# The hand-over into and out of the attention of a hybrid attention and RG-LRU block: other order of the first loads, other slots, earlier loads for the next stage

## The chip, the core and the metric

The kernel runs on one core of a Trainium2 chip. The metric is the device time of one launch in microseconds (us). The engines are TensorE (PE, matmuls; its weight loads are listed as PEld), VectorE (DVE), ScalarE (ACT), GpSimd (POOL) and SyncE (SP, which here only issues DMAs). Each engine works through its own instructions in the order in which the program writes them; engines wait for each other by semaphores. The tile framework is used with a manual schedule: the order on each engine is the order of the calls in the code.

## The reference

One decoder block over 2048 positions of width 1024:

```python
proj = x @ w_in + b_in            # q, k, v of 24 heads (3 groups of 8), g_attn, u_lru, g_lru, two merge gates
q, k = rope(q), rope(k)
for g, (window, dilation) in enumerate(((128, 1), (512, 4), (2048, 16))):
    # query t sees keys t - j*dilation, j = 0..128: blocks of 128 queries against [previous, own] block of keys
    o_g, lse_g = dilated_band_attention(q[:, :, g], k[:, :, g], v[:, :, g], window, dilation)
attn = sum(softmax(lse over g) * o_g) * silu(g_attn)
y_a  = attn @ w_attn_proj                                  # 512 -> 1024
h    = rg_lru(causal_depthwise_conv(u_lru), ...)           # scan over positions
y_b  = (h * silu(g_lru)) @ w_lru_proj                      # 1024 -> 1024
merged = sigmoid(gA) * y_a + sigmoid(gB) * y_b
out  = layer_norm(ALPHA * x + merged @ w_out + b_out)
```

## The kernel before

All products are float32 in accuracy: an operand is split into a high part in the format that PE multiplies in one pass (fp32r) and a low part, the rest, and a product is three matmuls (high x high, high x low, low x high). A split is one ACT activation (the high part) and one subtraction on DVE or POOL (the low part).

Four stages follow each other, with PE the busiest engine in each.

**Projection** (to 1463 us). Writes q (already split: `qh`, `ql`), k, v, the gates and h = the LRU's output times its gate to scratch tensors in device memory. In its last pieces of work (the counter j of the last sequence step) the dictionary `begin` (L882) issues the attention's first loads on SP.

**Attention** (1463 to 1768 us). There are 12 units u = 0..11; a unit is a group g = (0, 2, 1)[u % 3] with two of its heads (a pair hp = u // 3), over 16 blocks of 128 queries. The main loop (L1071) takes a pair of blocks each round, its index j being 8 a unit. A round writes, in this order: the tasks that have come due (`run(late)`), the score products of this pair (`scores`, PE, L953), `weigh` of its first block (DVE adds the mask and takes the row's minimum, L966; ACT takes the exp, L968), the PE transposes of the p of the round two before (`turn_p`, L982) and their copies out of PSUM (`copy_p`, ACT L995, every third time also ACT, else DVE L997, for the second half), `weigh` of the second block, and the products with V of the round three before (`values`, L1013). A finished group of four blocks goes to `o_scr` by a POOL DMA. The counter `now["n"]` rises by one with each block, so by two a round; `later(lag, fn)` puts fn on a list that `run(late)` calls when lag blocks have gone by.

A unit needs three things: q (`A`, 2 MB in four transfers, `q_parts` L811), raw k (`C`, 1 MB in two transfers, `k_parts` L780), split into `B` and the rest in place (`k_split`, two pieces of a POOL cast L799 and a POOL subtraction L800; for unit 0 on ACT and DVE), and V (four transfers, `v_parts`; one V tile holds two head pairs of a group).

**yb** (1768 to 1970 us). 32 jobs n = 8c + f, `yb_job` L1214: chunk c of 512 positions, f a block of 128 output columns, 8 x 3 matmuls each (L1223 to L1225). Its weights W_f1 are loaded and split by `prep_wl(f)`, two splits of 128 x 512 a tile (L1043), its h by `load_h(c, k)`, one split each (L1040 and, for c = 0, the rest on POOL). `prep_wl(0)`, `prep_wl(1)` and `load_h(0, 0..7)` are called in unit 11 of the attention, the others in this stage, `prep_wl(f)` for f = 2..7 at job f - 2. Beside it run the 16 `combine` calls, that normalise and add the three groups' o (DVE L1150, POOL L1152 to L1154), transpose them on PE (L1159) and gate them. In the last jobs the next stage's operands are prepared: `prep_wa`, `prep_wo` and `load_at`.

**ya and output** (1970 to 2228 us). `ya_job` (L1298 to L1300), the merge, `out_job` with W_out, and the layer norm.

The large tiles live in slots of fixed size, X0 to X5 for the whole program, Y0 to Y3 for the attention, Z0 to Z3 after it. A tile that takes a slot waits, at its first write, for the last reader of the tile that had it before. The tenants named in this text:

- `QSLOT` (X3, X1, Y0) and `KSLOT` (X4, Y3) for A and B; `VSLOT` (L760) for V; raw k (`KR`, L777) in X2 and X5 by turns, two units to a tile.
- `prep_wl` (L1048): W_f1 tiles f = 0, 1 in X2, then 2, 3 in X0, 4, 5 in X1, 6, 7 in X5.
- `prep_wo` (L1183): W_out tiles in Z2 (k = 0, 1), X0 (2, 3), X1 (4, 5), X5 (6, 7). Job 28 is the first to call it for k = 2.

Raw loads pass through `rc` tiles (L1035), 4 buffers in the attention.

```python
    def prep_wo(k, j):
        if k % 2 == 0 and j == 0:
            WO["t"] = big(("Z2", "X0", "X1", "X5")[k // 2], [P, 2, 2, D], F32R, f"wo{k}")
```

Of the kernel before, what the change touches and what calls it, by code (L numbers as in the profile page):

```python
# [8 lines left out]
F32 = mybir.dt.float32  # L9
F32R = mybir.dt.float32r  # L10
# [5 lines left out]
P = 128  # L16
S = 2048
# [14 lines left out]
def hybrid_block_kernel(ctx: ExitStack, tc: tile.TileContext, a: dict, out: bass.AP):  # L32
# [73 lines left out]
    def later(lag, fn):  # L106
        late.append((now["n"] + lag, fn))
# [649 lines left out]
    at(base[len(seq)] + 12, lambda: load_cs(1))  # L757

    QSLOT, KSLOT = ("X3", "X1", "Y0"), ("X4", "Y3")
    VSLOT = {(0, 0): "X0", (2, 0): "Y1", (1, 0): "Y2", (0, 1): "X0", (2, 1): "Y1", (1, 1): "Y2"}  # L760
    KR = {}

    units = {}
# [5 lines left out]
    def k_parts(u):  # L769

        g, hp = unit(u)
        src = qk_scr["k", 4 * g + hp].rearrange("(d h) s -> h d s", h=2)

        def part(h, hs):
            def fn():
                if h == 0 and u % 2 == 0:
                    KR["t"] = big(("X2", "X5")[u // 2 % 2], [P, 2, S], F32R, f"C{u}")  # L777
                if h == 0:
                    units[u] = [None, None, KR["t"][:, u % 2]]
                sp.dma_start(flat(units[u][2][hs]), src[h])  # L780
            return fn

        return [part(0, lo_), part(1, up_)]
# [95 lines left out]
            at(max(t, 0), fn)  # L879

    firstv = v_parts(0, 0)
    begin = {0: k_parts(0), 1: q_parts(0), 2: k_parts(1), 4: firstv[:1], 5: firstv[1:]}  # L882
    low = NS
    where = [(s, j) for s in range(NQ) for j in range(ticks[s])]
    for T, (s, j) in enumerate(where):
# [147 lines left out]
    cur = {"rc": at_p}  # L1033

    def rc(name):  # L1035
        return cur["rc"].tile([P, CH], F32, tag="rc", name=name, bufs=(4 if cur["rc"] is at_p else 6))

    def split(h, l, r, scale=None, eng=dve):
        if scale is None:
# [3 lines left out]
            act.activation(h, r, AF.Copy, scale=scale)  # L1043
            dve.scalar_tensor_tensor(out=l, in0=r, scalar=scale, in1=flat(h), op0=ALU.mult, op1=ALU.subtract)

    def prep_wl(f):
        if f % 2 == 0:
            WL["t"] = big(("X2", "X0", "X1", "X5")[f // 2], [P, 2, 2, 8, P], F32R, f"wl{f}")  # L1048
        t = WL[f] = WL["t"][:, f % 2]
        for j in range(2):  # L1050
            ks = slice(4 * j, 4 * j + 4)
            r = rc(f"wlr{f}{j}").rearrange("p (k f) -> p k f", f=P)
            sp.dma_start(r, a["w_f1"][f, :, 4 + 4 * j:8 + 4 * j, :])
            later(1, lambda r=r, ks=ks: split(t[:, 0, ks], t[:, 1, ks], r, 0.5))

    def load_h(c, k):
        if k % 4 == 0:
            HH["t"] = big((("X3", "X4"), ("Z0", "Z1"))[c % 2][k // 4], [P, 4, 2, CH], F32R, f"h{c}{k}")
        t = HH[c, k] = HH["t"][:, k % 4]
        r = rc(f"hr{c}{k}")  # L1060
        sp.dma_start(r, hb_scr[k * P:(k + 1) * P, c * CH:(c + 1) * CH])
        eng = pool if c == 0 else dve
        later(1 if c else 2, lambda: split(t[:, 0], t[:, 1], r, eng=eng))

    NB = 12 * 16
    for fn in q_parts(1) + v_parts(2, 0) + k_parts(2):
        fn()
# [3 lines left out]
    for j in range(NJ + 3):  # L1071
        u, n0 = divmod(2 * j, 16)
        run(late)
        if j < NJ:
            scores(j)
            weigh(2 * j)
        if 2 <= j < NJ + 2:
            turn_p(j - 2)
            copy_p(j - 2, 0)
            copy_p(j - 2, 1)  # L1080
        if j < NJ:
            weigh(2 * j + 1)
        if j >= 3:
            values(j - 3)
        for n in (n0, n0 + 1):
            if 1 <= n <= 2 and u <= 10:
                k_split(u + 1, n - 1)
            if n == 0 and 1 <= u <= 9:
                loads += k_parts(u + 2)
            if n == 0 and u <= 9:  # L1090
                loads += q_parts(u + 2)
            if n == 7 and u in VORD:
                loads += v_parts(*VORD[u])
            if loads:
                loads.pop(0)()
            if u == 11 and n in (1, 2):
                prep_wl(n - 1)
            if u == 11 and 3 <= n < 11:
                load_h(0, n - 3)
            now["n"] += 1  # L1100
            if n == n0:
                run(late)
# [357 lines left out]
```

## Time and profile before

| | |
|---|---|
| runs before | 2216.63, 2217.81, 2247.49 us (median 2217.81) |
| profiled execution | 2229.57 us; span of the profile 2227.8 us |
| mean granted TensorE clock over the span | 0.986 of full speed |

| stage | us | PE busy us | granted clock | DMA share |
|---|---|---|---|---|
| projection | 0 to 1463 | 1452.18 | 1.00 | 0.75 |
| attention | 1463 to 1768 | 297.54 | 0.91 | 0.77 |
| yb | 1768 to 1970 | 199.99 | 0.99 | 0.80 |
| ya and output | 1970 to 2228 | 246.48 | 0.99 | 0.40 |

The granted clock is the rate that the chip's throttle allows TensorE, as a share of full speed. The DMA share is the mean busy share of the core's 16 DMA engines. In the rows below, a line of the timeline reads: start in us, length in us, engine, source line, operation, written tile <- read tiles, shapes, count, and in brackets the idle time just before with what ended it. A row of the windows view reads: stretch, its length, then busy time and count of PE, PEld, DVE, ACT and POOL, then the granted clock, the DMA share and the GB/s moved.

### The profile page before, as it was taken

What the parts mean: (1) busy time and instruction counts of PE and PEld (TensorE: products, weight loads), DVE (VectorE), ACT (ScalarE), POOL (GpSimd) and SP (SyncE); (2) the same over time, 40 slices, a digit from 0 to 9 for tenths busy, and PEclk for the clock granted to TensorE, in tenths of its full rate; (3) what the DMA queues carried; (4) which work ended last, traced back from release to release, by engine and by line L of the source; (5) the groups of instructions that cost most, each with busy time, mean ns of one, the idle gap of its engine ahead of it and who ended that gap; (6) DMA issues with size and microseconds to landing.
All of it is one profiled execution on the core that took longest, in us unless ns stands there. A gap on an engine that the chain in (4) does not pass through costs nothing. (4 is left out here: it accounts for less than half of the span.)

```text
span 2227.8 us, 35342 instructions
## 1 busy us (share of the span) xinstructions
PE 2196.2 (99%) x12016; PEld 1848.7 (83%) x12016; DVE 1742.7 (78%) x3242; ACT 1198.4 (54%) x2171; POOL 715.4 (32%) x559
## 2 busy tenths in 40 slices
PE   8999999999999999999999999999999999999998
PEld 6888888888887888888888888889999878888786
DVE  7888898899998777787788878747776377877677
ACT  5456466656566566667677776647776411121100
POOL 1555455455554011111111111114433246621220
PEclk9999999999999999999999999989999699999999
DMA  6977977977977766586576776699984389864431
GB/s 211 261 233 213 273 229 222 273 216 247 278 235 224 254 193 200 187 231 191 185 216 195 229 204 209 209 260 280 263 240 121 124 293 291 254 215 146 156 123 66
DMA packets 295524, 481.75 MB, mean 216 GB/s; under 512 B 90176, under 2 KB 122976, under 8 KB 290736
## 3 DMA queue, kind: packets, MB, share of 16 engines
q1 hardware_dynamic: 275888, 437.61, 63.4%
q0 software_dynamic: 14128, 32.19, 7.0%
q10 hardware_dynamic: 5328, 9.70, 1.2%
q8 instruction: 95, 1.56, 0.3%
q14 instruction: 85, 0.70, 0.1%
HBM read 303.17 MB, written 176.23 MB: 215 GB/s over the span
## 5 line engine op out<-in xcount | busy, mean ns | idle before, releaser
L614 PE MATMUL q<-xT,hS 128*128 128x512 f32 x1632 | 503.9, 390 | 1.3 <-DVE y L230 1.3
L614 PE MATMUL q<-xB,hA 128*128 128x512 f32 x1344 | 417.3, 392 | 9.1 <-ACT xB L218 8.5
L614 PE MATMUL q<-xT,l 128*128 128x512 f32 x1088 | 423.6, 389 | 0.0
L614 PE MATMUL q<-xB,l 128*128 128x512 f32 x944 | 368.4, 390 | 0.0
L614 PEld LDWEIGHTS q<-xT,hS 128*128 128x128 f32 x1632 | 305.4, 188 | 64.5 <-issue 1.7
L614 PEld LDWEIGHTS q<-xB,hA 128*128 128x128 f32 x1344 | 252.3, 189 | 62.3 <-ACT xB L218 8.5
L614 PEld LDWEIGHTS q<-xT,l 128*128 128x128 f32 x1088 | 204.2, 188 | 42.7
L614 PEld LDWEIGHTS q<-xB,l 128*128 128x128 f32 x944 | 177.7, 188 | 37.4
L968 ACT ACTIVATE p<-p,osb 128x256 f32<-128x256 f32 (+1 forms) x384 | 154.9, 453 | 87.3 <-DVE osb L966 86.7
L230 POOL TENSOR_TENSOR sw<-sw,sin 128x512 f32<-128x512 f32 x96 | 153.7, 1623 | 122.6 <-ACT sw L318 99.7
L230 POOL TENSOR_TENSOR y<-y,h 128x512 f32<-128x512 f32 x28 | 40.2, 1437 | 412.8 <-DVE h L517 336.8
L1013 PE MATMUL o<-V,ptb 128*128 128x65 f32 x1200 | 169.7, 297 | 2.5 <-DMA V<-v_scr 2.5
L614 PE MATMUL q<-xB,hS 128*128 128x512 f32 x544 | 168.6, 391 | 0.3 <-DVE v L230 0.3
L614 PE MATMUL q<-xT,hA 128*128 128x512 f32 x544 | 168.1, 390 | 0.1
L1013 PEld LDWEIGHTS o<-V,ptb 128*128 128x128 f32 x1200 | 156.2, 208 | 9.4 <-DMA V<-v_scr 2.6
L966 DVE CUSTOM_DVE_ANT_0 p<-s,mask 128x256 f32<-128x256 f32 (+1 forms) x384 | 121.7, 362 | 46.7 <-PE s L953 46.5
L274 ACT ACTIVATE hA<-wA 128x512 fp32r<-128x512 f32 x220 | 138.7, 635 | 21.2 <-PE g L483 6.6
L274 ACT ACTIVATE hS<-S 128x512 fp32r<-128x512 f32 x170 | 108.5, 638 | 61.9 <-DVE S L230 55.0
L230 POOL TENSOR_TENSOR l<-wA,hA 128x512 fp32r<-128x512 f32 x68 | 107.9, 1587 | 81.5 <-ACT hA L274 58.6
L614 PEld LDWEIGHTS q<-xT,hA 128*128 128x128 f32 x544 | 101.7, 188 | 21.4 <-issue 0.5
L614 PEld LDWEIGHTS q<-xB,hS 128*128 128x128 f32 x544 | 101.3, 188 | 21.3 <-issue 0.7
L230 DVE TENSOR_TENSOR y<-y,cos 128x512 f32<-128x512 f32 x96 | 106.6, 1117 | 0.0
(197 smaller groups left out, 4651.9 us busy)
## 6 DMA issues: line engine op xcount, KB each, us to landing
wA<-in_w_in_dram SPq DMA_DIRECT2D x219, 256.0 KB, 4.6
wl_scr<-l SPq DMA_DIRECT2D x102, 512.0 KB, 4.9
l<-wl_scr SPq DMA_DIRECT2D x102, 512.0 KB, 4.0
wS<-in_w_in_dram SPq DMA_DIRECT2D x102, 256.0 KB, 4.1
wS<-in_w_in_dram POOLq DMA_DIRECT2D x68, 256.0 KB, 7.2
mg_scr<-y SPq DMA_DIRECT2D x59, 256.0 KB, 4.9
o_scr<-osb POOLq DMA_DIRECT2D x48, 264.0 KB, 8.0
oc<-o_scr SPq DMA_DIRECT2D x48, 264.0 KB, 4.9
```

What stands on the lines that cost most here:

```text
L230: eng.tensor_tensor(out=out, in0=in0, in1=in1, op=op)
L274: act.activation(heads(h), heads(r, False), AF.Copy)
L614: pe.matmul(bank, w[:, ks], x[:, kk, xx], start=(first and i == 0), stop=(last and i == 11))
L966: dve.tensor_tensor_reduce(out=p[:, h, lo:256], in0=bank[h][:, m % 2, lo:256], in1=mask[:, lo:256], scale=1.0, scalar=3e38, op0=ALU.add, o ...
L968: act.activation(p[:, h, lo:256], p[:, h, lo:256], AF.Exp, scale=-1.0, bias=mm)
L1013: pe.matmul(o[:, b, h * 65:h * 65 + 65], ptb[:, b, 2 * h + x, :], V[:, kb, vo + h * 65:vo + h * 65 + 65], start=(x == lo // P), stop=(x == 1))
```

## The change

It has four parts.

1. The first loads. `begin` issues V for unit 0 ahead of unit 1's raw k. So that V need not wait for a slot that is still in use, V of group 0 moves from X0 to X5, and the raw k tiles that used X5 move to X0.
2. The copies of p. In rounds j = 2, 3, 4 of the attention, `weigh` of the pair's first block comes behind `turn_p` and `copy_p`, not ahead of them.
3. The next stage's first operands. `prep_wl` can do one half of a tile (`js`); the halves of W_f1 tile 0 are called in unit 10, as are the first four `load_h`; the other four `load_h` and tile 1 are called in unit 11. Each call stands in a round of its own, and its split follows six blocks (three rounds) behind the load, where it was one or two blocks. `rc` has 5 buffers in place of 4 in the attention.
4. W_f1's tiles exchange slots: f = 2, 3 in X5, f = 6, 7 in X0. `prep_wo`'s table is as before.

```diff
-    VSLOT = {(0, 0): "X0", (2, 0): "Y1", (1, 0): "Y2", (0, 1): "X0", (2, 1): "Y1", (1, 1): "Y2"}
+    VSLOT = {(0, 0): "X5", (2, 0): "Y1", (1, 0): "Y2", (0, 1): "X5", (2, 1): "Y1", (1, 1): "Y2"}
...
-                    KR["t"] = big(("X2", "X5")[u // 2 % 2], [P, 2, S], F32R, f"C{u}")
+                    KR["t"] = big(("X2", "X0")[u // 2 % 2], [P, 2, S], F32R, f"C{u}")
...
-    begin = {0: k_parts(0), 1: q_parts(0), 2: k_parts(1), 4: firstv[:1], 5: firstv[1:]}
+    begin = {0: k_parts(0), 1: q_parts(0), 3: firstv[:2], 4: firstv[2:], 5: k_parts(1)}
...
-        return cur["rc"].tile([P, CH], F32, tag="rc", name=name, bufs=(4 if cur["rc"] is at_p else 6))
+        return cur["rc"].tile([P, CH], F32, tag="rc", name=name, bufs=(5 if cur["rc"] is at_p else 6))
...
-    def prep_wl(f):
-        if f % 2 == 0:
-            WL["t"] = big(("X2", "X0", "X1", "X5")[f // 2], [P, 2, 2, 8, P], F32R, f"wl{f}")
-        t = WL[f] = WL["t"][:, f % 2]
-        for j in range(2):
+    def prep_wl(f, js=(0, 1)):
+        if js != 1:
+            if f % 2 == 0:
+                WL["t"] = big(("X2", "X5", "X1", "X0")[f // 2], [P, 2, 2, 8, P], F32R, f"wl{f}")
+            WL[f] = WL["t"][:, f % 2]
+        t = WL[f]
+        ahead = js in (0, 1)
+        for j in (js,) if ahead else js:
...
-            later(1, lambda r=r, ks=ks: split(t[:, 0, ks], t[:, 1, ks], r, 0.5))
+            later(6 if ahead else 1, lambda r=r, ks=ks: split(t[:, 0, ks], t[:, 1, ks], r, 0.5))
...
-        later(1 if c else 2, lambda: split(t[:, 0], t[:, 1], r, eng=eng))
-
+        later(1 if c else 6, lambda: split(t[:, 0], t[:, 1], r, eng=eng))
+
+    ahead = {(10, 2): lambda: prep_wl(0, 0), (10, 4): lambda: prep_wl(0, 1),
+             (11, 8): lambda: prep_wl(1, 0), (11, 10): lambda: prep_wl(1, 1)}
+    for k in range(4):
+        ahead[10, 6 + 2 * k] = lambda k=k: load_h(0, k)
+        ahead[11, 2 * k] = lambda k=k: load_h(0, 4 + k)
...
             scores(j)
-            weigh(2 * j)
+            if j > 4:
+                weigh(2 * j)
         if 2 <= j < NJ + 2:
             turn_p(j - 2)
             copy_p(j - 2, 0)
             copy_p(j - 2, 1)
         if j < NJ:
+            if j <= 4:
+                weigh(2 * j)
             weigh(2 * j + 1)
...
-            if u == 11 and n in (1, 2):
-                prep_wl(n - 1)
-            if u == 11 and 3 <= n < 11:
-                load_h(0, n - 3)
+            if (u, n) in ahead:
+                ahead.pop((u, n))()
```

On SP, at the end of the projection, the queue reads as follows (A is q, C raw k, V the values; k_scr_106, qh_scr_104 and ql_scr_105 belong to unit 1).

```order
 L811 DMA A_13962<-qh_scr_80 64x2048 x2
 L811 DMA A_13962<-ql_scr_81 64x2048 x2
+L827 DMA V_14003<-v_scr_74 128x4x260 x4
 L780 DMA C_13942<-k_scr_106 64x2048 x2
-L827 DMA V_14023<-v_scr_74 128x4x260 x4
 L811 DMA A_14080<-qh_scr_104 64x2048 x2
 L811 DMA A_14080<-ql_scr_105 64x2048 x2
```

V's four transfers moved ahead of the two of unit 1's raw k; what stands ahead of unit 1's q is the same in sum.

On ACT, in round j = 2 of unit 0, the first one with copies of p (rows of L968 are exps, x2 for the two heads; rows of L995 copies out of PSUM), there stood before:

```order
L968 ACTIVATE p_14143<-p_14143,osb_14107 128x256 x2
L968 ACTIVATE p_14167<-p_14167,osb_14166 128x256 x2
L995 ACTIVATE ptb_14174<-pt_14172 128x2x64
L995 ACTIVATE ptb_14174<-pt_14172 128x4x64
L995 ACTIVATE ptb_14174<-pt_14173 128x2x64
L995 ACTIVATE ptb_14174<-pt_14173 128x4x64
L968 ACTIVATE p_14191<-p_14191,osb_14166 128x256 x2
```

And there stands now:

```order
L968 ACTIVATE p_14143<-p_14143,osb_14107 128x256 x2
L995 ACTIVATE ptb_14168<-pt_14166 128x2x64
L995 ACTIVATE ptb_14168<-pt_14166 128x4x64
L995 ACTIVATE ptb_14168<-pt_14167 128x2x64
L995 ACTIVATE ptb_14168<-pt_14167 128x4x64
L968 ACTIVATE p_14186<-p_14186,osb_14185 128x256 x2
L968 ACTIVATE p_14191<-p_14191,osb_14185 128x256 x2
```

The four copies moved ahead of the exps of the round's first block.

On ACT, at the first splits of W_f1 (L1043), which stood in unit 11 (the exps of 128x128 are blocks without a previous block):

```order
L1043 ACTIVATE wl_18694<-wlr_18695 128x512
L1043 ACTIVATE wl_18694<-wlr_18697 128x512
L968 ACTIVATE p_18718<-p_18718,osb_18664 128x128 x2
L995 ACTIVATE ptb_18725<-pt_18723 128x4x64
L995 ACTIVATE ptb_18725<-pt_18724 128x4x64
L968 ACTIVATE p_18736<-p_18736,osb_18664 128x128 x2
L1043 ACTIVATE wl_18694<-wlr_18747 128x512
L1043 ACTIVATE wl_18694<-wlr_18749 128x512
```

They now stand in unit 10, one in a round, followed by the first split of h (L1040):

```order
L1043 ACTIVATE wl_18382<-wlr_18383 128x512
L968 ACTIVATE p_18499<-p_18499,osb_18498 128x128 x2
L995 ACTIVATE ptb_18506<-pt_18504 128x4x64
L968 ACTIVATE p_18517<-p_18517,osb_18498 128x128 x2
L1043 ACTIVATE wl_18382<-wlr_18433 128x512
L968 ACTIVATE p_18547<-p_18547,osb_18498 128x128 x2
L995 ACTIVATE ptb_18554<-pt_18552 128x4x64
L968 ACTIVATE p_18565<-p_18565,osb_18498 128x128 x2
L1040 ACTIVATE h_18479<-hr_18480 128x512
```

The pair of splits ahead of a round's exps became a single one, and the last two W_f1 splits moved behind those of h, into unit 11's later rounds.

On ACT, at the first splits of W_out that go to X0 (wo_20748 is tiles 2 and 3, called from job 28 on), the rows are the same before and now:

```order
L1043 ACTIVATE wa_20745<-war_20746 128x512
L1040 ACTIVATE wo_20748<-wor_20749 128x512
L1040 ACTIVATE at_20693<-atr_20751 128x512
L1043 ACTIVATE wa_20745<-war_20811 128x512
L1040 ACTIVATE wo_20748<-wor_20813 128x512
L1040 ACTIVATE at_20693<-atr_20815 128x512
```

Nothing moved here; what changed is which tile of W_f1 had X0 before them: f = 2, 3 before, f = 6, 7 now.

## The prediction

> **What bounds the kernel now.** I read the page first, then TensorE's granted clock by stretches, then the rows at the places where it drops.
>
> ```profile
> PE 2196.2 (99%) x12016; PEld 1848.7 (83%) x12016; DVE 1742.7 (78%) x3242; ACT 1198.4 (54%) x2171; POOL 715.4 (32%) x559
> PEclk9999999999999999999999999989999699999999
> ```
>
> TensorE is busy 99% of the span, so only two things can give time: its idle microseconds, and the two slices (27 and 32 of 40) in which its clock was not full. The windows view resolves both; its first column after the stretch's length is PE's busy time, and PEclk follows the engines.
>
> ```profile
> 1460.00:1470.00 10.00, 8.04 (x76) 6.31 (x74) 6.53 (x30) 5.82 (x15) 1.94 (x4) 1.00 1.02 265
> 1470.00:1480.00 10.00, 7.17 (x60) 6.62 (x60) 3.31 (x14) 4.52 (x13) 6.42 (x4) 0.55 1.08 267
> 1480.00:1490.00 10.00, 10.00 (x68) 9.65 (x69) 3.06 (x15) 4.00 (x9) 0.79 (x1) 0.50 1.00 249
> 1490.00:1500.00 10.00, 10.00 (x128) 9.54 (x126) 6.01 (x28) 6.57 (x16) 0.76 (x1) 0.93 1.04 270
> ...
> 1710.00:1720.00 10.00, 10.00 (x129) 9.39 (x130) 6.46 (x39) 6.76 (x23) 1.32 (x2) 1.00 0.17 57
> 1720.00:1730.00 10.00, 9.30 (x116) 8.24 (x114) 7.07 (x34) 7.20 (x21) 1.09 (x2) 1.00 0.32 109
> 1730.00:1740.00 10.00, 8.02 (x83) 7.20 (x81) 6.77 (x34) 8.99 (x21) 6.07 (x6) 0.69 0.53 162
> 1740.00:1750.00 10.00, 10.00 (x64) 9.65 (x66) 4.33 (x16) 6.04 (x13) 5.02 (x5) 0.50 0.14 51
> ...
> 1770.00:1780.00 10.00, 10.00 (x43) 8.20 (x42) 2.50 (x4) 2.19 (x4) 0.00 (x0) 0.93 0.29 91
> ```
>
> Twice PE idles a little (1.96 + 2.83 us; later 0.70 + 1.98 us) and the clock falls to 0.50. In the first stretch it is back 0.07 x 10 / 0.5 = 1.4 us into the window 1490 to 1500, at 1491.4; in the second it falls 6.2 us before 1740, at 1733.8, and is back at 1771.4. So half clock outlasts its idle time by far, while PE shows 10.00 of 10. What a half-clock microsecond costs is read from PE's timeline, where one attention step (a pair of blocks) runs from one score product to the next:
>
> ```profile
> 1464.79 0.49 PE L953 MATMUL s<-B,A 64*128 64x128 f32 x3 [0.90 <-DMA A<-ql_scr]
> ...
> 1470.64 0.94 PE L982 MATMUL pt<-ident,p 64*128 64x64 f32 x15 [0.15 <-ACT ptb L995]
> 1474.04 2.82 PE L1013 MATMUL o<-V,ptb 128*128 128x65 f32 x12 [2.46 <-DMA V<-v_scr]
> 1476.79 0.58 PE L953 MATMUL s<-B,A 64*128 64x256 f32 x2
> 1482.83 0.58 PE L953 MATMUL s<-B,A 64*128 64x256 f32 x2
> 1488.87 0.58 PE L953 MATMUL s<-B,A 64*128 64x256 f32 x2
> 1493.26 0.39 PE L953 MATMUL s<-B,A 64*128 64x256 f32 x2
> 1496.59 0.33 PE L953 MATMUL s<-B,A 64*128 64x128 f32 x2
> ```
>
> A step takes 6.04 us at half clock (1482.83 to 1488.87) and 3.33 us at full (1493.26 to 1496.59): each half-clock microsecond of attention loses 1 - 3.33/6.04 = 0.45 us. Steps at full clock have no PE idle, so elsewhere the attention is PE-bound.
>
> **Edit 1: V before the second raw k, V in X5, p copies ahead of exps (steps 2 to 4).** The row at 1474.04 is the stall aimed at: PE waited 2.46 us for V's first quarter. V now starts as the first q ends at 1464.8; the two raw k transfers that used to come between ended when POOL's cast (below) could start, 4.9 us later. So V lands about 4.9 us sooner, at 1469. The transposes, which ended at 1471.6, were held by copies standing behind two exps; at the 0.40 us or so that an exp takes they end some 0.8 us sooner, at 1470.8. The V wait is gone, and from 1470.8 the rest of that step (1474.04 to 1476.79, 2.75 us at half clock, 1.5 at full) and four steps of 3.33 us bring unit 1's first scores to 1485.6, against 1496.6 now.
>
> What is late next? Unit 1's q. Its last transfer's issue and landing:
>
> ```profile
> L811 SPq DMA_DIRECT2D A<-ql_scr x2: 594/595/596, 1473.1 to 1473.8; - x2
> DMA to landing us min/median/max: 14.3/15.1/16.0
> ```
>
> It is issued at 1473.8 and lands 16.0 us later, at 1489.8. The DMA column above is 1.00 to 1.08 throughout, so the engines are the limit; the reorder leaves the same bytes ahead of this q (first k and q, second k, V). I take 1489.8 as fixed. The second raw k moves back by V's four transfers, to about when V's last landed, 1480.4, and POOL's split of it, two of each of these, follows:
>
> ```profile
> 1469.69 1.04 POOL L799 CAST B<-C 128x1024 fp32r<-128x1024 f32 x1 [3.95 <-DMA C<-k_scr]
> 1470.81 2.35 POOL L800 TENSOR_TENSOR C<-C,B 128x1024 fp32r<-128x1024 f32 x1
> ```
>
> 2 x (1.04 + 2.35) = 6.8 us: ready at 1487.2, hidden by the q. Queued behind it on POOL are only stores of o, which nobody waits for soon. So unit 1 starts at 1489.8, **6.7 us earlier** than now, after a PE idle of 1489.8 - 1485.6 = **4.2 us in one piece**. That is longer than any idle piece in the first stretch above, so I expect the clock to halve here. How long is unknown: after PE was back at 1474.0 it stayed half for 17.4 us; in the second stretch for 37.6 us, ended only when the dense products of the next stage began. I take the first, being the same unit's end: 17.4 x 0.45 = **+7.8 us**; bounds 0 and 37.6 x 0.45 = +16.9. Edit 1 in sum: -6.7 + 7.8 = +1.1 us.
>
> The Trainium skill, "TensorE: Matmul & The Clock Gate", section "What's actually happening", has the clock at full rate again after one busy window of about 3.4 us. The window 1480 to 1490 (busy 10.00, clock 0.50) speaks against it in attention; by it this term would be an estimated 3.4 x 0.45 = 1.5 us. That is a rival below.
>
> **Edit 2: weights and h one unit ahead, one split a step.** Now two ACT splits stand ahead of a step's exps, and PE waits for the copies behind them:
>
> ```profile
> 1724.16 1.13 ACT L1043 ACTIVATE wl<-wlr 128x512 fp32r<-128x512 f32 x2
> ...
> 1727.36 0.73 PE L982 MATMUL pt<-ident,p 64*128 64x64 f32 x8 [0.69 <-ACT ptb L995]
> ...
> 1731.61 0.46 PE L982 MATMUL pt<-ident,p 64*128 64x64 f32 x8 [1.58 <-ACT ptb L995]
> ```
>
> Afterwards one split of 0.57 us stands in a step. In the window 1710 to 1720 (unit 10) ACT is idle 3.24 us of 10, 0.7 us in each 2.2 us step: it fits. The two wl splits in unit 10 also put 0.69 us on DVE, ahead of the masks that ACT waits for; I allow 0.3 us of PE idle each, half of the 0.69 us that a pair costs above (bounds 0 and 0.69), far from what halved the clock. Their DMAs have three steps, 6.6 us, at a DMA share of 0.17 to 0.32; SP has no other load then. Unit 8 is of the same group as unit 11, so its length at full clock is known, and so is a tail step:
>
> ```profile
> 1494.07 0.65 PE L982 MATMUL pt<-ident,p 64*128 64x64 f32 x16
> 1494.66 2.00 PE L1013 MATMUL o<-V,ptb 128*128 128x65 f32 x16
> ...
> 1653.40 0.33 PE L953 MATMUL s<-B,A 64*128 64x128 f32 x2
> 1674.67 0.33 PE L953 MATMUL s<-B,A 64*128 64x128 f32 x2
> ...
> 1721.45 0.33 PE L953 MATMUL s<-B,A 64*128 64x128 f32 x2
> 1768.10 0.77 PE L1223 MATMUL yb<-h,wl 128*128 128x512 f32 x1
> ```
>
> Unit 11 and its tail take 46.6 us (1721.45 to 1768.10). They would take 21.3 us as unit 8 did, and 2 x 0.65 + 3 x 2.00 = 7.3 us of tail: 28.6. That is 18.0 us less, and the 3.3 us of half clock in the dense products gives 1.5 more; less 0.6: **-18.9 us**.
>
> **What the slot swap does later.** W_f1's last two tiles (f = 6, 7) now lie in X0, which the third and fourth W_out tiles still take at n = 28. Until now X0 held f = 2, 3, last read at n = 27; f = 7 is read to the end of n = 31. So ACT's first split into X0, and DVE's behind it, wait for PE to finish the yb stage. Behind them in order stand the next at split, yb's evacuation, and the combine's normalisation, which POOL and then PE's transposes need before ya:
>
> ```profile
> 1941.21 0.62 ACT L1040 ACTIVATE wo<-wor 128x512 fp32r<-128x512 f32 x1
> ...
> 1941.94 0.68 DVE L1041 TENSOR_TENSOR wo<-wor,wo 128x512 fp32r<-128x512 f32 x1
> ...
> 1945.22 4.33 POOL L1152 TENSOR_TENSOR oc<-oc,cE 128x512 f32<-128x512 f32 x3 [4.96 <-DVE cE L1150]
> 1949.52 1.31 POOL L1153 TENSOR_TENSOR oc<-oc 128x512 f32<-128x512 f32 x1
> 1950.90 1.63 POOL L1154 TENSOR_TENSOR oc<-oc 128x512 f32<-128x512 f32 x1
> ...
> 1953.67 0.40 PE L1225 MATMUL yb<-h,wl 128*128 128x512 f32 x1
> 1953.91 0.60 PE L1159 MATMUL ctp<-ident,oc 128*128 128x128 f32 x4
> ```
>
> Now that split runs at 1941.2, 12.9 us before yb ends at 1954.07; POOL is done at 1952.5 and the transposes start at 1953.9 unhindered. Afterwards the chain starts at yb's end: ACT 0.62, from DVE's split to POOL's start 1945.22 - 1941.94 = 3.28, POOL 7.3: 11.2 us. **+11.2 us of PE idle**; the loads and splits of `at` queued behind fit inside it. Such an idle halves the clock; dense products ended the second half-clock stretch 3.3 us after they began, so 3.3 x 0.45 = +1.5 us. Sum **+12.7 us** (bounds 0, were the slot free, and 11.2 + 7.8 = 19, with the longer tail of the first stretch).
>
> The fifth rc buffer and the other slots cost nothing: at those places PE is at 10.00 of 10.
>
> **Sum.** +1.1 - 18.9 + 12.7 = -5.1 us against the profiled execution (2229.57 us, span 2227.8). That execution is 11.8 us over the median of the runs, 2217.81, whose spread of 31 us may be half-clock stretches of other lengths; I carry the difference over: 2217.8 - 5.1 = **2212.7 us**. A measurement of this kernel tells no change from about 2%, 44 us.
>
> **Rivals.**
> - *The X0 wait costs nothing*, if ACT and DVE had slack there. For: ACT idles 9.68 us before that place. Against: POOL is done only 1.4 us before PE needs it. Then 2212.7 - 12.7 = 2200.
> - *Half clock in unit 1 ends at once.* For: it did in dense products. Against: five windows of 3.4 us at half clock above. Then 2212.7 - 6.3 = 2206.
> - *Half clock in unit 1 lasts.* Place: the q wait. Price: 0.45 us for each us over 17.4; from 29 us on (17.4 + 5.1/0.45) the kernel is slower than before. At 37.6 us it is 2222; if it ran through units 1 and 2 (their 42 us at full clock become 76), 2239; middle 2229. For: attention did not end the second stretch. Against: it ended the first.
> - *The change doesn't do what it says in units 10 and 11*: PE still waits and the clock halves. For: ACT and DVE are near full with a split in each short step. Against: half the load of now. Then 2212.7 + 18.9 = 2231.6.
>
> **How the numbers follow.** Forecast 0.47 (own range 2206 to 2219); X0 free 0.09; clock back at once 0.12; half clock lasts 0.22; unit 11 still halved 0.10. The range 2199 to 2236 leaves out the ends of the third and fourth rivals and combinations of the first two, under 0.2 in all. The 2% bounds lie at 2173.5 and 2262.2; no single case reaches them: faster 0.01, same 0.96, slower 0.03.
>
> **What would show it.** In the changed profile: no V wait at step 3; unit 1's first scores waiting about 4 us for ql, then PEclk 0.50; unit 11 at 1.00 with 3.3 us full steps; ahead of the first ya a PE idle of about 11 us ended by POOL's oc, and before it ACT and DVE idle some 12 us until yb's last product. I am wrong if the loads land much earlier, if short idles halve the clock in unit 10, or if the swap blocks more than this chain.

## The result and the profile after

| | median us | runs | lowest to highest |
|---|---|---|---|
| before | 2221.39 | 20 | 2214.12 to 2250.05 |
| changed | 2244.68 | 20 | 2221.12 to 2275.94 |

The ratio is 1.0085, with a 95% interval of 1.0064 to 1.0106 (it leaves out the runs more than 1.5% above the fastest of their kernel, which the table keeps): some 19 us slower by the ratio, 23 by the medians. The forecast was 2212.7 us, within 2199 to 2236; the median lies 32.0 us above the forecast and 8.7 us above the range. The changed kernel's profiled execution took 2239.05 us, span 2237.2.

From the page of the changed kernel, the rows of section 1 and of TensorE's granted clock in 40 slices:

```profile
PE 2197.9 (98%) x12016; PEld 1849.8 (83%) x12016; DVE 1744.2 (78%) x3242; ACT 1197.8 (54%) x2171; POOL 716.3 (32%) x559
PEclk9999999999999999999999999977999999999999
```

TensorE's work is the same. The slice at unit 11 is full again, but the weak slice at the start has become two. TensorE's timeline of the changed kernel at the start of the attention, then at unit 8 and at the parts that follow:

```profile
1469.82 0.71 PE L982 MATMUL pt<-ident,p 64*128 64x64 f32 x15 [0.15 <-ACT ptb L995]
1470.46 1.55 PE L1013 MATMUL o<-V,ptb 128*128 128x65 f32 x12
...
1485.28 0.33 PE L953 MATMUL s<-B,A 64*128 64x128 f32 x2
1487.21 0.49 PE L953 MATMUL s<-B,A 64*128 64x128 f32 x3 [1.38 <-DMA A<-ql_scr]
...
1667.72 0.33 PE L953 MATMUL s<-B,A 64*128 64x128 f32 x2
...
1730.46 0.47 PE L982 MATMUL pt<-ident,p 64*128 64x64 f32 x8 [0.29 <-ACT ptb L995]
1733.49 0.46 PE L982 MATMUL pt<-ident,p 64*128 64x64 f32 x8 [0.61 <-ACT ptb L995]
1737.14 0.33 PE L953 MATMUL s<-B,A 64*128 64x128 f32 x2
1766.31 0.48 PE L1232 MATMUL yb<-h,wl 128*128 128x512 f32 x1
1962.05 1.11 PE L1168 MATMUL ctp<-ident,oc 128*128 128x128 f32 x4 [11.28 <-POOL oc L1163]
```

V's wait is gone (1470.46 has no bracket), and unit 1's first scores start at 1485.28. They then wait 1.38 us for q. The windows of the same profile show what follows (columns as before: PE, PEld, DVE, ACT, POOL, granted clock, DMA share):

```profile
1470.00:1480.00 10.00, 10.00 (x143) 9.54 (x141) 6.96 (x30) 8.42 (x20) 0.99 (x1) 1.00 1.04 270
1480.00:1490.00 10.00, 8.62 (x98) 8.14 (x94) 5.66 (x28) 6.06 (x15) 7.23 (x6) 0.88 1.03 310
1490.00:1500.00 10.00, 10.00 (x70) 9.65 (x71) 2.48 (x11) 2.44 (x7) 1.30 (x2) 0.50 1.02 317
...
1530.00:1540.00 10.00, 10.00 (x71) 9.41 (x72) 4.88 (x21) 5.06 (x14) 2.84 (x2) 0.50 1.02 252
1540.00:1550.00 10.00, 10.00 (x126) 9.54 (x124) 6.80 (x29) 7.06 (x16) 0.54 (x1) 0.89 0.30 89
```

The clock falls at 1487.7 (0.88 in that window: 2.4 us at half) and is back at 1542.3: 54.6 us, through unit 1 and into the fifth of unit 2's eight rounds. Unit 8 began at 1653.40 before and begins at 1667.72 now, **14.3 us later**; the yb stage began at 1768.10 and begins at 1766.31, so units 8 to 11 give 16.1 back; the span ends 9.4 us later.

### The profile page after: what moved, and what is told of

The parts are those of the page before. It is cut to its first block, busy times and chain, and to the rows that moved or that the text cites. A ratio compares the mean times of both kernels' runs of the same rounds, so it can differ in the third digit from the quotient of the medians.

```text
span 2237.2 us, 35336 instructions
## 1 busy us (share of the span) xinstructions
PE 2197.9 (98%) x12016; PEld 1849.8 (83%) x12016; DVE 1744.2 (78%) x3242; ACT 1197.8 (54%) x2171; POOL 716.3 (32%) x559
## 4 chain that ended last, share of the span: by engine, by line
PE 87%; issue 4%; DVE 3%; DMA 3%; ACT 2%; POOL 1%; SPq 0%; ACTq 0%; POOLq 0%; DVEq 0%
PE q L614 59%; PE o L1013 6%; PE s L953 4%; PE yb L1234 3%; PE yb L1232 3%; PE yb L1233 3%; PE pt L982 2%; PE z L1346 1%; PE z L1345 1%; PE z L1344 1%; PE vtp L366 1%; POOL me L1315 1%; DMA A<-ql_scr 1%; DMA V<-v_scr 1%; PE g L484 1%
## 5 line engine op out<-in xcount | busy, mean ns | idle before, releaser
L968 ACT ACTIVATE p<-p,osb 128x256 f32<-128x256 f32 (+1 forms) x384 | 154.9, 454 | 95.7 <-DVE osb L966 95.4
L1013 PE MATMUL o<-V,ptb 128*128 128x65 f32 x1200 | 167.3, 294 | 0.0
L1013 PEld LDWEIGHTS o<-V,ptb 128*128 128x128 f32 x1200 | 153.6, 205 | 7.1
```

Of the source, the lines that this page charges most:

```text
L968: act.activation(p[:, h, lo:256], p[:, h, lo:256], AF.Exp, scale=-1.0, bias=mm)
L1013: pe.matmul(o[:, b, h * 65:h * 65 + 65], ptb[:, b, 2 * h + x, :], V[:, kb, vo + h * 65:vo + h * 65 + 65], start=(x == lo // P), stop=(x == 1))
```

## The experiments

The "kernel with matched slots" below is the changed kernel with one line exchanged. TensorE's half clock is read from the windows as above; "x of y runs" are single times.

### Taking the change apart

**x0_matched**

```diff
-            WO["t"] = big(("Z2", "X0", "X1", "X5")[k // 2], [P, 2, 2, D], F32R, f"wo{k}")
+            WO["t"] = big(("Z2", "X5", "X1", "X0")[k // 2], [P, 2, 2, D], F32R, f"wo{k}")
```

> The changed kernel with W_out's slot table exchanged in the same way as W_f1's (k = 2, 3 in X5, k = 6, 7 in X0), so that no W_out split waits for the end of yb. Theory: the 11.28 us of TensorE idle ahead of the first ya of the changed profile, and the 10.2 us of half clock in it, are the slot wait and nothing else; both go, and the kernel is 12 to 13 us under the changed one (about 2232 us where that has 2244.7). Rival: the wait is that of the combine itself, which comes late for another reason (ACT and DVE behind in yb); then the idle stays at 8 us or more and less than 4 us are gained. The start of unit 1, untouched, should wait 1.4 us for q and run at half clock through units 1 and 2 as in the changed kernel.

Median 2233.33 us, ratio to before 1.0023 [0.9983, 1.0063]: 11.4 us under the changed kernel by the medians, 14 by the ratios. No idle piece above 0.15 us is left between yb and ya. Unit 1 still waits 1.34 us for q, and the clock is half from 1487.6 for 71.7 us. The slot wait is one line's price, and the rest of the loss is at the start.

**splits_only** (part 3 on the kernel before)

```diff
+    ahead = {(10, 2): lambda: prep_wl(0, 0), (10, 4): lambda: prep_wl(0, 1),
...
-            if u == 11 and n in (1, 2):
-                prep_wl(n - 1)
```

> The kernel before with part 3 alone (splits of W_f1 and h a unit ahead, one a round, fifth rc buffer); slots, first loads and p copies as before. Theory: the start stays as before (V waited for about 2.5 us, some 20 us of half clock in unit 0), unit 11 runs at full clock, and the kernel is 16 to 19 us under the one before (about 2204 us where that has 2221). Rival: the clock falls wherever the program has had full clock for long, so that a half stretch turns up elsewhere in units 8 to 11 or in yb, and the gain is under 6 us.

Median 2216.35 us, ratio 0.9972 [0.9938, 1.0007]: some 4 to 6 us, not 18, with an interval that just includes no gain. Its windows from unit 10 on:

```profile
1720.00:1760.00 40.00, 38.78 (x449) 35.63 (x450) 25.61 (x117) 30.03 (x78) 14.43 (x16) 1.00 0.48 154
```

Unit 11 is at full clock, as forecast, and no half stretch turned up elsewhere behind the start, so the rival falls too. What is wrong is the size (last experiment below).

**head_only** (parts 1 and 2 on the kernel before, with V in X5 and raw k in X0)

```diff
-    begin = {0: k_parts(0), 1: q_parts(0), 2: k_parts(1), 4: firstv[:1], 5: firstv[1:]}
+    begin = {0: k_parts(0), 1: q_parts(0), 3: firstv[:2], 4: firstv[2:], 5: k_parts(1)}
...
-            weigh(2 * j)
+            if j > 4:
+                weigh(2 * j)
```

> The kernel before with parts 1 and 2 alone (first loads, p copies, V in X5, raw k in X0); splits and later slots as before. Theory: the wait of unit 1 for its q, about 1.4 us at the start of a unit of short steps, halves the clock, and the clock stays half through units 1 and 2, about 55 us: 14 us slower than the kernel before (about 2235 us where that has 2221), unit 11 as before with its half clock. Rival of the prediction on record: the half clock ends with the 17 us it had in unit 0, and the kernel is within 3 us of the one before. Second rival: the half clock of units 1 and 2 comes from something in the later parts of the change; then units 1 and 2 are at full clock here and the kernel is about 11 us faster than before.

Median 2247.97 us, ratio 1.0072 [1.0032, 1.0113]: 16 us slower by the ratio, 27 by the medians, so the start alone does it. In its profile q was later still, and in units 1 and 2 the clock fell twice, not once for some 55 us as expected: at unit 1's q, for 10.2 us, and in unit 2, for 23.9 us.

```profile
1490.93 0.32 PE L953 MATMUL s<-B,A 64*128 64x128 f32 x1 [2.79 <-DMA A<-ql_scr]
1493.52 0.79 PE L953 MATMUL s<-B,A 64*128 64x128 f32 x3 [2.27 <-DMA A<-ql_scr]
1522.98 0.69 PE L982 MATMUL pt<-ident,p 64*128 64x64 f32 x8 [2.25 <-ACT ptb L995]
```

By the ratios the three parts add up in this order: start +0.0072, splits -0.0049 (1.0023), slot +0.0062 (1.0085), so +16, -11 and +14 us; each ratio is known to some 0.004, or 9 us, and by the medians the parts are +27, -15 and +10. The profiles' terms are +14.3, -17.6 and +12.7.

### Is it the wait for q that halves the clock?

**filler** (on the kernel with matched slots)

```diff
+        if j == 8:
+            W = units[0][0]
+            for i in range(4):
+                pe.matmul(bank[i % 2].rearrange("p b f -> p (b f)"), W[:, 0, 0:P], W[:, 0, 0:CH], start=True, stop=True)
```

> The kernel with matched slots, and four extra products of 128 x 512 on TensorE ahead of unit 1's first scores, into the PSUM banks that these scores then overwrite (about 1.6 us at 0.39 us each): they add work and change no load. Theory: it is the idle time while q is on its way that halves the clock; filled, the clock stays full in units 1 and 2, unit 3 starts about 25 us earlier than in the kernel with matched slots, and the kernel takes about 25 us less than that one. Rival: the clock falls by a budget of time or power, and more work brings it down at least as surely; then the half clock stays at about 55 us and the time is the same or 1 to 2 us longer.

It decides nothing. The four products took 1.17 us, q landed later in this run, and TensorE waited all the same:

```profile
1487.83 0.33 PE L957 MATMUL s<-B,A 64*128 64x128 f32 x1 [0.38 <-DMA A<-ql_scr]
1490.00 0.50 PE L957 MATMUL s<-B,A 64*128 64x128 f32 x3 [1.84 <-DMA A<-ql_scr]
```

The clock was half for 58 us; median 2231.91 us, as with matched slots alone.

**filler12** (against the filler)

```diff
-            for i in range(4):
+            for i in range(12):
```

> As the filler of four products, which left TensorE waiting 0.38 and 1.84 us for q all the same, with twelve (4.7 us at 0.39 us each), more than the whole wait. Theory (idle time halves the clock): no wait is left, the clock stays full in units 1 and 2, unit 1 begins 2 to 3 us later than with matched slots alone and unit 3 about 20 us sooner; about 2212 us. Rival (a budget of work or power brings the clock down): half clock of 50 us or more although TensorE was never idle; 2235 us or more.

```profile
1486.45 3.00 PE L941 MATMUL s<-A 128*128 128x512 f32 x12
1489.38 0.33 PE L957 MATMUL s<-B,A 64*128 64x128 f32 x2
...
1490.00:1500.00 10.00, 10.00 (x131) 9.59 (x130) 5.07 (x29) 5.55 (x16) 0.00 (x0) 1.00 1.03 310
1500.00:1510.00 10.00, 10.00 (x133) 9.39 (x130) 6.85 (x44) 7.21 (x24) 7.59 (x6) 1.00 1.01 238
1510.00:1520.00 10.00, 7.84 (x77) 7.12 (x78) 3.66 (x25) 4.39 (x15) 1.76 (x3) 0.76 1.03 333
```

The timeline's scores have no wait, and the windows show full clock through unit 1, with 3 us more work in it: in this profile the idle time is the cause, not a budget of work. Then unit 2 waits in its turn (0.48 us for its q, 1.69 us for copies) and the clock falls there, for 23.9 us. Median 2221.84 us, ratio 0.9979 [0.9943, 1.0015], 10 to 11 us under matched slots; the 2212 expected leaves out unit 2's wait.

**half_v** (on the kernel with matched slots)

```diff
-                    sp.dma_start(V[:, 4 * i:4 * i + 4], src[i * CH:(i + 1) * CH].rearrange("(n p) f -> p n f", p=P))
+                    sp.dma_start(V[:, 4 * i:4 * i + 4, cs], src[i * CH:(i + 1) * CH].rearrange("(n p) f -> p n f", p=P)[:, :, cs])
...
-    firstv = v_parts(0, 0)
+    firstv = v_parts(0, 0, slice(0, 130))
...
+            if n == 0 and u == 1:
+                loads += v_parts(0, 0, slice(130, 260))
```

> The kernel with matched slots, and V's first transfers halved: a V tile holds the values of two head pairs, and unit 0 reads only the first. Its half (130 of 260 columns, four transfers) stays at V's place, the other half comes with unit 1's loads; unit 3 is the first to read it. So 1.07 MB less stand ahead of unit 1's q, about 4 us at the 265 GB/s that the trace shows there, and q lands about 2 us ahead of unit 1's first scores. Theory (the wait for q halves the clock in units 1 and 2): no wait, full clock, about 25 us under the kernel with matched slots, about 2208 us where that has 2233 and the kernel before 2220. Rival (the clock falls there whether PE waits or not): half clock in units 1 and 2 as before, within 3 us of the kernel with matched slots. If halved rows of 520 bytes move at half the rate, q is not sooner, and this run tells nothing of either.

Median 2213.69 us, ratio 0.9965 [0.9930, 1.0000]: 20 us under matched slots by the medians, 13 by the ratios. Unit 1 has no wait and full clock. In unit 2 VectorE waits for a buffer of o whose store is still on its way, the copies stand behind, and TensorE waits (rows of DVE and of PE):

```profile
1509.98 0.29 DVE L966 CUSTOM_DVE_ANT_0 p<-s,mask 128x128 f32<-128x128 f32 x1 [2.98 <-DMA o_scr<-osb]
...
1511.33 0.69 PE L982 MATMUL pt<-ident,p 64*128 64x64 f32 x8 [1.86 <-ACT ptb L995]
```

The clock is half for 17 us from there.

### What ends a half-clock stretch?

**burst** (against the filler)

```diff
-        if j == 8:
+        if j == 10:
...
-            for i in range(4):
+            for i in range(10):
```

> The kernel with matched slots, and ten extra products of 128 x 512 ahead of the scores of unit 1's third round (j = 10), inside the stretch at half clock, where such a product takes 0.77 us: 7.7 us of added dense work. Theory (in the attention the half clock outlasts its cause because the mix of the attention, above all the products with V of 65 columns, doesn't bring the clock back, while dense products do): the clock is back at full within 4 us of the burst's end, the half stretch is 20 to 25 us in place of 55 to 72, which gives back 15 us or more and costs 7.7: 5 to 15 us under the kernel with matched slots. Rival (the half clock lasts its own time, whatever runs): the stretch is 55 us or more and the kernel 5 to 8 us slower than with matched slots.

Median 2214.40 us, all 12 runs within 2209.34 to 2219.63, where the kernel with matched slots ranges from 2210.85 to 2261.93. But in the profiled run the clock came back at 1499.9, before the burst began at 1501.0, so that profile doesn't show the burst at work.

**burst9** (against the burst)

```diff
-        if j == 10:
+        if j == 9:
```

> The kernel with matched slots, and ten extra products of 128 x 512 ahead of the scores of unit 1's second round (j = 9), about 6 us behind the fall of the clock. Theory (the mix decides): the clock is back at the end of the first or second window of 3.41 us that holds the dense products, the half stretch is 7 to 14 us, and all runs lie together near 2212 to 2216 us. Rival (a stretch lasts its own time): half clock of 50 us or more in the profile, and runs up to 2240 us and more as with matched slots alone.

```profile
1490.66 0.79 PE L957 MATMUL s<-B,A 64*128 64x128 f32 x3 [2.08 <-DMA A<-ql_scr]
1496.09 4.38 PE L941 MATMUL s<-A 128*128 128x512 f32 x10
...
1490.00:1500.00 10.00, 9.34 (x48) 8.43 (x49) 1.36 (x9) 2.24 (x6) 0.00 (x0) 0.50 1.04 314
1500.00:1510.00 10.00, 10.00 (x128) 9.20 (x128) 5.07 (x29) 5.12 (x16) 6.62 (x5) 1.00 1.01 219
```

The same wait, the same fall, and the clock is back at 1500.1, at the end of the first piece of 3.41 us that held nothing but dense products. All 12 runs lie within 2209.30 to 2213.94 us. Extra work thus makes the kernel faster than matched slots alone, by 21 us by the medians and 14 by the ratios (0.9960 against 1.0023). This one profile could be chance, since the stretch in head_only also ended after 10.2 us, without such products; the stronger evidence is the twelve runs, each with a mean granted clock of 0.996, where those with matched slots have 0.970 to 0.996.

**The mix.** The half stretches in the attention, in all 18 profiles of this case, are multiples of 3.41 us (20.5, 37.6, 54.6 and so on). I cut them into pieces of that length and gave each instant on TensorE to the instruction last begun. Of the pieces in the attention without idle time and without dense products, **125 had more than 0.40 of their time in the products with V (L1013), and none of them was the last of its stretch; 43 had less, and 28 of these were.** The bound was chosen after the count (one ending piece lies at 0.40, and the pieces that go on start again at 0.41), and 13 of the 28 are single pieces at the start of unit 0 that hold no product with V at all. So this is a pattern in the profiles, not a rule of the chip. In the changed kernel, the V products' rows alone (first number: their busy time on PE):

```profile
1514.98:1518.40 3.42, 1.49 (x8) 1.30 (x8) 0.50 0.99 305
1518.40:1521.81 3.41, 1.48 (x8) 1.29 (x7) 0.50 0.82 301
...
1535.46:1538.88 3.42, 1.75 (x8) 1.75 (x8) 0.50 1.05 280
1538.88:1542.29 3.41, 1.04 (x6) 0.86 (x6) 0.50 0.89 222
1542.29:1545.70 3.41, 2.07 (x19) 1.93 (x18) 1.00 0.30 112
```

The pieces in the short rounds hold 1.48 us of 3.41 or more (0.43 of busy time, 0.41 by the last instruction begun), and the stretch goes on; the one with 1.04 (0.30) is its last. The short rounds are the eight of unit 1 and the first two of unit 2, whose blocks have no previous block. A long round of unit 0 takes 6 us at half clock, and some piece falls mostly on its scores and transposes; a short round takes 3.9 us, about a piece, and each piece has the same mix. So a fall in unit 0 could end there, and a fall at the start of unit 1 that has not ended with unit 0's last products with V lasts until unit 2's long rounds. Of the five profiles with a fall at unit 1's start and no dense products ahead of its end, three show that (the changed kernel, x0_matched, filler); in two the clock was back ahead of the short rounds (head_only after 10.2 us, burst after 13.7). Why 15 of the 43 did not end it is open, and so is what the chip counts.

### Is the median's run the profiled one?

**before_again** (no edit: the kernel before once more)

> The kernel before, unchanged, for a second profile of it. The prediction took the half clock of unit 11 (37.55 us) from one profiled execution of 2229.57 us, 8 to 12 us over the median. Theory: in an execution near the median (2217 to 2222 us) TensorE waits in unit 11 as in that profile (about 2.7 us in three pieces), but the clock there stays full or is back within 10 us, which is why part 3 alone gave some 4 us and not 18. Rival: unit 11 runs at half clock here too, and part 3 lost its gain elsewhere.

This execution took 2252.66 us, far from the median, so the question stayed open. It shows how far the start of the kernel before varies: the same V wait,

```profile
1474.98 2.82 PE L1013 MATMUL o<-V,ptb 128*128 128x65 f32 x12 [2.20 <-DMA V<-v_scr]
...
1540.00:1550.00 10.00, 10.00 (x76) 9.41 (x75) 4.69 (x27) 4.45 (x14) 4.34 (x4) 0.50 1.01 222
1550.00:1560.00 10.00, 10.00 (x102) 9.44 (x102) 5.79 (x27) 6.06 (x16) 1.10 (x2) 0.66 0.78 210
```

but half clock for 81.9 us, through units 0 to 2, and 20.5 us more in unit 11.

The clocks on record narrow the question. The profiled execution's mean of 0.986 is 2 x 0.014 x 2228 = 62 us at half clock. The runs of the kernel before that took 2217 to 2222 us have means of 0.989 to 0.994, an estimated 27 to 49 us. So a run near the median had 13 to 35 us less of it than the execution from which part 3 was sized. Where in the program that was, no trace shows.

### A calm base, and each part on it

**base** (half_v, and)

```diff
-            st["osb"] = at_p.tile([P, 4, 132], F32, tag="osb", name=f"osb{m}", bufs=6)
+            st["osb"] = at_p.tile([P, 4, 132], F32, tag="osb", name=f"osb{m}", bufs=8)
-        p = at_p.tile([P, 2, 256], F32, tag="p", name=f"p{m}", bufs=8)
+        p = at_p.tile([P, 2, 256], F32, tag="p", name=f"p{m}", bufs=6)
```

> The kernel with halved first V transfers and matched slots, with 8 buffers in place of 6 for the o blocks on their way to memory (and 6 in place of 8 for p, to make room). In the profile with halved V the one wait left in units 1 to 3 is VectorE's 2.98 us for a store of o to land, which made TensorE wait 1.86 us in unit 2 and halved the clock for 17 us. Theory: with two more buffers nobody waits for that store, the clock stays full from unit 1 to the end of the attention, and 1.9 + 17 x 0.45 = 9.5 us go: about 2204 us where that has 2213.7, and the runs lie closer together. Rival: the next late transfer (a q or V of units 2 and 3) takes the place of the store, and less than 3 us are gained.

Median 2214.39 us (2202.88 to 2249.13), ratio 0.9959 [0.9915, 1.0003]. The store's wait is gone; the rival holds, since unit 2's q comes late in its place, and the clock falls for 13.7 us:

```profile
1508.79 0.44 PE L953 MATMUL s<-B,A 64*128 64x128 f32 x3 [1.51 <-DMA A<-ql_scr]
```

**base_x0** (against the base: the changed kernel's W_out table)

```diff
-            WO["t"] = big(("Z2", "X5", "X1", "X0")[k // 2], [P, 2, 2, D], F32R, f"wo{k}")
+            WO["t"] = big(("Z2", "X0", "X1", "X5")[k // 2], [P, 2, 2, D], F32R, f"wo{k}")
```

> The same base, with W_out's slot table as in the changed kernel (k = 2, 3 in X0): the slot wait alone, on a base whose start is calm. Theory: 11.3 us of idle time ahead of the first ya and 10 us of half clock in and behind it, +12 to +13 us on the base. Rival: part of it is covered, under +8 us.

Median 2228.17 us, 13.8 over the base (11 by the ratios), with the same idle piece to the digit:

```profile
1949.39 1.11 PE L1170 MATMUL ctp<-ident,oc 128*128 128x128 f32 x4 [11.28 <-POOL oc L1165]
```

**base_p_back** (against the base: part 2 undone)

```diff
-            if j > 4:
-                weigh(2 * j)
+            weigh(2 * j)
```

> The same base with part 2 undone (copies of p behind the exps of the round's first block in rounds 2 to 4, as before the change). Theory: the transposes of round 3 stand some 0.8 us later, nothing else, 0 to 1 us. Rival: the added idle time in unit 0, on top of the wait for q at its start, brings the clock down for 10 us or more there, +5 us or more.

Median 2209.51 us against 2214.39, both with runs beyond 2235: inconclusive, and repeated below.

**base_old_splits** (against the base: part 3 undone, both slot tables as before the change)

```diff
-            if (u, n) in ahead:
-                ahead.pop((u, n))()
+            if u == 11 and n in (1, 2):
+                prep_wl(n - 1)
+            if u == 11 and 3 <= n < 11:
+                load_h(0, n - 3)
```

> The same base with part 3 undone: the splits of W_f1 and h in unit 11 as before the change, W_f1 and W_out slots as before it. It tells what part 3 is worth without the noise of the start. Theory of the prediction: TensorE waits 2.7 us in unit 11, the clock is half for 20 to 40 us from there: +10 to +19 us on the base. Rival (part 3 alone moved the median by 4 us only): in most runs the clock is back soon, +2 to +6 us.

Median 2223.07 us, +8.7 (6 by the ratios). Three of 12 runs took 2206.76 to 2208.38, the others 2217.80 and more; the profiled one (2222.34) had the clock at half for 44.4 us from 1719. The worth of part 3 is of two kinds, and the base was too restless to weigh them.

**best** (against the base: unit 1's V tile halved as well)

```diff
-    for fn in q_parts(1) + v_parts(2, 0) + k_parts(2):
+    for fn in q_parts(1) + v_parts(2, 0, slice(0, 130)) + k_parts(2):
...
+            if n == 0 and u == 2:
+                loads += v_parts(2, 0, slice(130, 260))
```

> The calm base (halved V for unit 0, 8 o buffers), with unit 1's V halved as well, the other half with unit 2's loads: another 1.07 MB, about 4 us, less ahead of unit 2's q, for which unit 2 waited 1.51 us. Theory: that wait is the last one that brings the clock down in units 1 to 10; without it 2203 to 2206 us in most runs, clock full from 1471 us to the end of the attention. Rival: V's halved rows (520 bytes in place of 4 x 1040 in one piece) or the next load come late in its place, and the time stays at 2210 us or more.

Median 2203.49 us, all runs within 2202.89 to 2207.19; **ratio 0.9922 [0.9900, 0.9943], 17 us under the kernel before** (15 by the medians). The whole attention in one window:

```profile
1463.00:1768.00 305.00, 300.85 (x3667) 280.83 (x3666) 201.31 (x953) 209.32 (x546) 115.46 (x102) 1.00 0.85 237
```

The clock is 1.00 throughout, and yb begins at 1742.8, 25.3 us sooner than in the profile of before.

**best_p_back** (best with part 2 undone, the diff of base_p_back)

> The same with part 2 undone. Theory: part 2 moves the transposes of unit 0's third round by under 1 us and nothing else, so the two medians are within 2 us. Rival: it decides whether the clock falls in unit 0; then they differ by 5 us or more.

Median 2203.97 us, 0.5 us more: part 2 is worth nothing that can be measured.

**best_old_splits** (best with part 3 undone, the diff of base_old_splits)

> The kernel without waits in units 1 to 10 (both first V tiles halved, 8 o buffers, runs within 4 us of each other), with part 3 undone: W_f1's and h's first splits in unit 11, two in one round, slots as before the change. Theory: TensorE's waits in unit 11 (1.7 us in the profile of the base with old splits) always cost 2 to 5 us, and in most runs the clock falls there and stays half until the yb stage, 28 to 45 us, for 12 to 18 us more: median 2218 to 2223, a few runs near 2207. Rival: the clock falls there only now and then; median under 2210, part 3 worth 5 us or less.

Median 2208.65 us, ratio 0.9962 [0.9942, 0.9983], so +5.2 us on best by the medians, 9 by the ratios. Five of nine runs took 2206.06 to 2208.65, four 2216.15 to 2221.58. In the profiled one (2206.06) TensorE waited 0.85 and 1.35 us in unit 11, and the clock was half for only 6.8 us, from 1720.4, when only the first of the two waits had passed:

```profile
1718.23 0.73 PE L982 MATMUL pt<-ident,p 64*128 64x64 f32 x8 [0.85 <-ACT ptb L995]
...
1710.00:1720.00 10.00, 9.15 (x115) 8.27 (x114) 6.57 (x33) 7.96 (x24) 1.10 (x2) 1.00 0.31 109
1720.00:1730.00 10.00, 8.65 (x93) 7.92 (x94) 7.37 (x34) 8.73 (x22) 5.55 (x5) 0.66 0.45 143
```

The rival of this run holds in the median: part 3 saves some 4 us in five runs of nine, and some 15 in the four whose mean granted clock was lower (0.990 to 0.993, against 0.995 to 0.996).

## Why the prediction was wrong, step by step

**Edit 1, the loads: mostly right.** V did not wait, and unit 1 began at 1485.28 (forecast 1485.6). The q was not fixed at 1489.8: its last transfer was issued at 1469.4 and not at 1473.8, took 17.8 us in place of 16.0, and landed 2.6 us sooner, so the idle piece was 1.38 us and not 4.2. Taking "the same bytes ahead" for the same landing was a wrong step, though it made the case look worse. (The 6.7 us by which unit 1 was to start earlier are 6.8 by the prediction's own rows, which changes nothing.)

**Edit 1, the half clock: the step that failed.** That the clock falls here was forecast. Its length was taken as the 17.4 us that it had lasted in the first stretch, "being the same unit's end"; it was 54.6 us in the profiled run, and edit 1 came to +14.3 us in place of +1.1. The price of a microsecond was right: 54.6 x 0.45 = 24.6 us, less the 9.9 us by which unit 1 stood ahead after its wait (1496.59 before; 1485.28 and 1.38 of waiting now), is 14.7. The neighbour in time was the wrong one to take the length from. As far as the pieces show, what counts is which instructions follow the fall: behind 1487 come unit 0's last products with V and then ten short rounds, and 125 pieces with such a share of these products ended no stretch. A short stretch seems to occur, but seldom: 3 of the changed kernel's 20 runs took 2221.12 to 2226.51 us at mean clocks of 0.991 to 0.994, where the profiled one has 0.984. The rival "half clock in unit 1 lasts" named the place and even "through units 1 and 2" at 2239 us, with too small a chance, 0.22 in all. The rule of the Trainium skill weighed there ("TensorE: Matmul & The Clock Gate", "What's actually happening"), full rate after one busy window, is contradicted by those 125 pieces and agrees with the dense piece of burst9.

**Edit 2 (part 3): right mechanism, a size from the wrong run.** Unit 11 did go to full clock, and in the profiles the term is 17.6 us: 16.1 up to yb, and 1.5 in it, against 18.9. Unit 10 took 1.4 us more (unit 11 begins 15.7 us later than before, unit 8 had begun 14.3 later), of which 0.6 was forecast. But the profile of before was a run with 37.55 us of half clock in unit 11. The prediction noted that it lay 11.8 us above the median, and then carried that difference over to the result as if it were a constant. On the median run part 3 is worth 4 to 5 us, by the ratios 6 to 9 (splits_only, best_old_splits). This and the failed step of edit 1 both moved the result up.

**The slot swap: right in every step.** The changed kernel's rows of ACT, POOL and PE at the end of yb:

```profile
1950.81 0.63 ACT L1040 ACTIVATE wo<-wor 128x512 fp32r<-128x512 f32 x1 [12.88 <-PE yb L1234]
...
1954.76 4.32 POOL L1161 TENSOR_TENSOR oc<-oc,cE 128x512 f32<-128x512 f32 x3 [17.87 <-DVE cE L1159]
...
1960.39 1.60 POOL L1163 TENSOR_TENSOR oc<-oc 128x512 f32<-128x512 f32 x1
```

The split waits for yb's last product, POOL's chain begins 3.95 us behind the split's start, and TensorE idles 11.28 us (forecast 11.2). The span's offset goes from -3.3 us at yb's end (1954.07 before, 1950.77 now) to +9.4: +12.7, as forecast.

**The sum.** +14.3 - 17.6 + 12.7 = +9.4 us between the two profiled executions; +19 us between the kernels by the ratio, +23 by the medians. Of the 32 us between the forecast and the median, 14.5 lie in the sum (+9.4 in place of -5.1), 3.6 in the median of the kernel before (2217.8 on three runs, 2221.4 on twenty), and some 14 in the two profiled executions: that of before took 8.2 us more than its median, that of the changed kernel 5.6 us less. By the mean clocks the first had more half clock than most runs of its kernel, so more to win from part 3, and the second a little less (0.984, against 0.981 to 0.983 in the runs of 2243 to 2247 us).

## What to carry to other kernels

A short wait of the bounding engine costs what comes after it: before moving it, look at which work follows, and whether that work has ever brought the clock back. Where runs of one kernel differ by more than the terms of the sum, a stall's size in one profiled execution is not its worth; look first where that execution stands among the runs. And two tables that hand the same slots on, here W_f1's and W_out's, are changed together: one unchanged line cost 11 to 14 us.

## What the runs showed of the hardware

Idle pieces of 0.85 us (best_old_splits) to 1.86 us (half_v) were enough to halve TensorE's clock. The Trainium skill ("TensorE: Matmul & The Clock Gate", "What's actually happening") has it fall after an idle window of about 3.4 us; these pieces are far shorter. Not each such piece does it: at the start of unit 0, 1.68 us in the profile of best and 1.54 us in that of the changed kernel left the clock at full. At half clock TensorE shows itself 100% busy, and the stretch can outlast its cause some fifty times (1.34 us of idle time, 71.7 us of half clock in x0_matched). Ten products that compute nothing of use, placed 6 us behind the fall (burst9), made the kernel 14 to 21 us faster and its runs even: 4.6 us from the lowest to the highest, in place of 51.
